# q norm and layer norm: two channel tiles added before the ones-matmuls, and a short last key tile in the first query half

## The chip, the cores and the metric

The kernel runs on one core of a Trainium2 chip, in one launch. Its time is that of the device, in microseconds (us), the median of several runs. A core has five engines with queues of their own: PE (TensorE, matmuls), DVE (VectorE), ACT (ScalarE), POOL (GpSimd) and SP (SyncE, which here only issues DMAs). PE reads SBUF and writes PSUM; it runs a matmul as a weight load (the stationary operand, "PEld" in the profile) and a pass of the moving operand.

## The reference

One layer of a hybrid decoder: 16 meta tokens are put ahead of 1024 tokens of width 1024, one input projection feeds four token mixers, their outputs are gated and merged, and an output projection is added to the residual. Float32 throughout. What the change touches are three pieces of it:

```python
# multi-head latent attention: norm of the low-rank query (256 channels), causal softmax
q = (rms_norm(c_q, q_norm_g) @ w_uq).reshape(b_, l_, MLA_HEADS, QK_NOPE + QK_ROPE)
...
s = jnp.where(k_pos[None, :] <= q_pos[:, None], s, -jnp.inf)
p = jax.nn.softmax(s, axis=-1)

# Conformer convolution module (256 channels)
z = causal_dwconv(z, w_dw) + b_dw
z = layer_norm(z, ln_g, ln_b)
```

`rms_norm` divides by the root of the mean of squares over the channels; `layer_norm` first takes the mean over the channels off.

## The kernel before

Most matrices lie with channels on the 128 partitions and tokens along the free dimension, so 256 channels are two tiles, and the 1024 tokens are worked in two halves of 512 (`c` = 0, 1). A float32 product is made of three matmuls of high and low parts (`split` makes these: ACT copies the high part, POOL or DVE subtracts it).

**Stage one** is the input projection, in units of seven block products each (tiles `ps_pa` to `ps_pd`; operands `A`, `S` from the weights, `B`, `T` from the input). `prep` turns the next weights into such operands (tiles `raw`, `ss`, `S`, `A` on DVE, ACT and POOL). Between the products, `pump` lets four "lanes" of smaller tasks take steps: the convolutions, the query and key/value tasks (`task_q`, `task_kv`), the short convolution, layer norm and pooling (`task_short`, `task_norm`, `task_pool`), and the output weights (`task_w`). `task_norm(1)` is the last task of its lane. Its last stores (`store_bo`, tile `cgt`, with `bohi`) are the last DMAs that SP issues for the stage.

**Column sums.** Sums over channels run across partitions, so PE makes them with a vector of ones. `rs_row` (line 849) takes a list `sqs` of tiles of squares, makes for each 128 tokens a matmul with the squares as the stationary operand and the ones as the moving one (one column), with all tiles of the list accumulated in one PSUM group; DVE scales, POOL takes the power -1/2 (tile `rs`), and PE transposes the result back into a row over all partitions. `task_q` (tile `sqq`, each half once) and `task_norm` (tile `lsq`, each half once) call it with two tiles, `task_kv` with one. `task_norm` also needs the sum of the values themselves: the convolution's output is loaded into two tiles `lacc`, and two matmuls of 512 columns, with ones as weights, put the sum on all partitions (`pa`). DVE takes the mean off `lacc`, ACT squares the result into `lsq`. Its tiles come from a ring of four (`t2`).

**Stage two** is attention, head by head and half by half, with the output products of the other three mixers as filling work (tiles `whl`, `bo`, `th`, `ps_y`). `maxima` makes a bound for each query's scores. `attend` (line 1330) goes over tiles of 128 keys, `nj` = 5 in the first half and 9 in the second: three score matmuls with the keys as weights (`ps_s`), the causal mask on DVE, exp on ACT (`p`), a split (`pt`), three value matmuls (`ps_o`). Keys count the 16 meta tokens, so the last tile of either half meets only the last 16 queries of the half. **Stage three** is the product of attention's output and the output projection.

**Order.** Every operation is recorded first, with a cost from a small model; `Plan.flush` then simulates the engines and writes out an order for each, once for each stage. An operation is taken when its inputs are planned to be ready and its buffers free, in the order of recording, where some (`plan.ahead`) are lifted. Loads and stores are given planned landing times, with some microseconds more inside `plan.slow`. The hardware keeps that order on each engine and waits where the plan was too early. The cost of a matmul in the model goes by its free size and not by the number of keys. All operations are issued in `issue`, so the profile shows line 330 for them; its groups are told apart by tile names.

Of the kernel before, what the change touches and what calls it, by code (L numbers as in the profile page):

```python
# [30 lines left out]
P = 128  # L31
D = 1024
NT = 1024
NM = 16
# [30 lines left out]
def f(ap):  # L65
    return ap.bitcast(F32)
# [369 lines left out]
def trunk_kernel(ctx, tc, a):  # L436
    nc = tc.nc
    plan = Plan(nc)
    PE, ACT, DVE, POOL, SP = (plan.engine(e) for e in ("PE", "ACT", "DVE", "POOL", "SP"))
# [7 lines left out]
    def ld(out, in_):  # L447
        SP.dma_start(f(out) if out.dtype == F32R else out, f(in_) if in_.dtype == F32R else in_)

    def copy(out, in_, scale=1.0):  # L450
        ACT.activation(out, in_, AF.Copy, scale=scale)
# [4 lines left out]
    def add(eng, out, x, y):  # L456
        eng.tensor_tensor(out, x, y, op=ALU.add)

    def mul(eng, out, x, y):
        eng.tensor_tensor(out, x, y, op=ALU.mult)  # L460

    def split(hi, lo, src, eng=None):
        copy(hi, src)
        sub(eng or POOL, lo, src, f(hi))
# [5 lines left out]
    ones = const.tile([P, 1], F32, name="ones")  # L470
# [44 lines left out]
    def bank(tag="x"):  # L515

        return psum.tile([P, 512], F32, tag=tag, bufs=2 if tag == "x" else 1, name=f"ps_{tag}")
# [10 lines left out]
    def t2(shape, dt=F32, name="t2"):  # L528
        return tp.tile(shape, dt, tag="t2", bufs=4, name=name)
# [4 lines left out]
    def col(shape, name):  # L534
        return tp.tile(shape, F32, tag=name, bufs=2 if name == "rs" else 1, name=name)
# [313 lines left out]
    def rs_row(sqs, of, scale=None, tag="x"):  # L849

        n = sqs[0].shape[1]
        p = min(n, P)
        pc = bank(tag)[:p, :n // p]
        for j in range(n // p):
            for i, sq in enumerate(sqs):
                PE.matmul(pc[:, j:j + 1].in_order(), sq[:, p * j:p * (j + 1)], ones, start=(i == 0),
                          stop=(i == len(sqs) - 1), skip_group_check=True)  # L860
        yield
        rs = col([P, 4], "rs")[:p, :n // p]
        DVE.tensor_scalar(rs, pc, 1.0 / of, EPS, op0=ALU.mult, op1=ALU.add)
        POOL.tensor_tensor(rs, rs, mhalf[:p, :n // p], op=ALU.pow)
        if scale:
            DVE.tensor_scalar(rs, rs, scale, None, op0=ALU.mult)
        yield
        out = bank(tag)[:, :n]
        for j in range(n // p):
            PE.transpose(out[:, p * j:p * (j + 1)], rs[:, j:j + 1].to_broadcast([p, P]), ident[:p, :p])  # L870
        yield
        return out
# [28 lines left out]
    def store_bo(i, c, src):  # L901

        s_ = slice(512 * c, 512 * (c + 1))
        hi, lo = t2([P, 512], F32R, name="bohi"), src.bitcast(F32R)
        split(hi, lo, src)
        ld(bo_dram[i][:, 0, s_], hi)
        ld(bo_dram[i][:, 1, s_], lo)

    def task_norm(c):

        s_ = slice(512 * c, 512 * (c + 1))
        acc = [t2([P, 512], name="lacc") for m in range(2)]
        for m in range(2):
            ld(acc[m], acc_dram[m][:, s_])
        pa = bank("y")
        for m in range(2):
            PE.matmul(pa, ones.to_broadcast([P, P]), acc[m], start=(m == 0), stop=(m == 1))
        yield
        sq = [t2([P, 512], name="lsq") for m in range(2)]
        for m in range(2):  # L920
            DVE.scalar_tensor_tensor(acc[m], pa, -1.0 / 256.0, acc[m], op0=ALU.mult, op1=ALU.add)
            ACT.activation(sq[m], acc[m], AF.Square)
        yield
        rs = yield from rs_row(sq, 256, tag="y")
        for m in range(2):
            g, b, hb = (t_[:, r + m:r + m + 1] for t_, r in ((par, R_LG), (par, R_LB), (par, R_HLB)))
            DVE.scalar_tensor_tensor(acc[m], acc[m], g, rs, op0=ALU.mult, op1=ALU.mult)
            th, cg = t2([P, 512], name="lth"), t2([P, 512], name="cgt")
            ACT.activation(th, acc[m], AF.Tanh, scale=0.5, bias=hb)
            ld(cg, z_dram[f"cg{m}"][:, s_])  # L930
            DVE.tensor_scalar(acc[m], acc[m], b, 0.5, op0=ALU.add, op1=ALU.mult)
            DVE.scalar_tensor_tensor(acc[m], th, 1.0, acc[m], op0=ALU.add, op1=ALU.mult)
            yield
            mul(POOL, cg, acc[m], cg)
            store_bo(2 + m, c, cg)
            yield
# [72 lines left out]
    def task_q(c):  # L1009
# [4 lines left out]
        for m in range(2):  # L1014
            ld(cq[:, m], z_dram[f"cq{m}"][:, s_])
            ACT.activation(sq[:, m], cq[:, m], AF.Square)
        yield
        rs = yield from rs_row([sq[:, 0], sq[:, 1]], 256, QK ** -0.5)
        ch = []
        for m in range(2):  # L1020
# [63 lines left out]
    def task_kv():  # L1084
# [20 lines left out]
        for n0, n in CH_KV:  # L1105
            rs = yield from rs_row([sq[:, n0:n0 + n]], P)
            DVE.scalar_tensor_tensor(ckv[:, n0:n0 + n], ckv[:, n0:n0 + n], par[:, R_KVG:R_KVG + 1], rs,
                                     op0=ALU.mult, op1=ALU.mult)
# [60 lines left out]
    def lane(*tasks):  # L1169

        for needs, task, *args in tasks:
# [3 lines left out]
            while True:  # L1175
# [10 lines left out]
             ): 0.8,  # L1186
        lane(*[((f"b{m}", f"c{m}", f"x{m}", f"sg{m}"), task_short, m, c) for m, c in halves]
             + [(("conv00", "conv10", "cg0", "cg1"), task_norm, 0)]
             + [((f"pv{m}", f"pg{m}"), task_pool, m, c) for m, c in halves]
             + [(("conv01", "conv11"), task_norm, 1)]): 1.1,  # L1190
        lane(*[((), task_w, n, i, c) for n in w_dram for i in range(len(w_dram[n][0])) for c in range(KD)]): 0.5,
    }
# [137 lines left out]
    def attend(h, c):  # L1330

        q_, k_, v_ = qt[h, c], kt[h % 2], vt[h % 2]
        po = bank("o")
        nj = 4 * c + 5
        for j in range(nj):
            lo_ = max(512 * c, P * j - NM)
            n = 512 * (c + 1) - lo_
            kn = P if j < 8 else NM
            ks = slice(P * j, P * j + kn)
            qs = slice(512 - n, 512)  # L1340
            s = bank("s")[:kn, :n]
            PE.matmul(s, k_[:NA, 0, ks], q_[:NA, 0, qs], start=True, stop=False)
            PE.matmul(s, k_[:QK, 0, ks], q_[:QK, 1, qs], start=False, stop=False)
            PE.matmul(s, k_[:QK, 1, ks], q_[:QK, 0, qs], start=False, stop=True)
            d0 = P * j - NM
            dl, dh = max(d0, 512 * c, 0), min(d0 + P, 512 * (c + 1))
            if dh > dl:
                sd = s[:, dl - lo_:dh - lo_]
                add(DVE, sd, sd, maskT[:kn, dl - d0:dh - d0])
            p32 = at.tile([P, 512], F32, tag="p32", bufs=3, name="p32")[:kn, :n]  # L1350
            pt_ = at.tile([P, 2, 512], F32R, tag="pt", bufs=4, name="pt")[:kn, :, :n]
            ACT.activation(p32, s, AF.Exp)
            split(pt_[:, 0], pt_[:, 1], p32)
            o = po[:, lo_ - 512 * c:]
            PE.matmul(o, v_[:kn, j, :P], pt_[:, 0], start=(j == 0), stop=False, skip_group_check=True)
            PE.matmul(o, v_[:kn, j, :P], pt_[:, 1], start=False, stop=False, skip_group_check=True)
            PE.matmul(o[:64], v_[:kn, j, P:], pt_[:, 0], start=False, stop=(j == nj - 1), skip_group_check=True)
            yield
        if c == 0:
            ol[h] = at.tile([P, 2, 512], F32, tag="ol", bufs=2, name="ol")  # L1360
        copy(ol[h][:, c], po)
# [111 lines left out]
    for i, (h, c) in enumerate(seq):  # L1473
        with plan.behind():
            if i + 2 < len(seq):
                load_q(*seq[i + 2])
            if c == 0 and h + 1 < H:
                load_kv(h + 1)
            if c == 0 and h % 2:
                smg[h] = at.tile([P, NT], F32, tag="smg", name="smg")  # L1480
                ld(smg[h], z_dram[f"mg{h // 2}"])
        for _ in attend(h, c):
            units += 1
            lead_to(-1, min(5 + units * 10 / 14, 5 * (i + 3)))
            refill()
        lead_to(i + 1)

        with plan.ahead(300 if h == H - 1 else 0):
            if h == H - 1:
                head_out(h, c, sums_pe(h, c))  # L1490
            elif c:
                for k, rb in enumerate(sums(h)):
                    head_out(h, k, rb)
# [233 lines left out]
```

## Time and profile before

| | |
|---|---|
| runs, us | 1011.25, 1011.64, 1013.38 (median 1011.64) |
| profiled execution: first to last instruction (span), us | 1010.7 |
| mean granted clock of TensorE | 0.993 |
| DMA over the span | 203.13 MB, 201 GB/s |

The time that the profiled execution takes besides its span isn't in the profile; the median of the runs is 0.9 us above the span. Times in the profile are microseconds from the first instruction, those of one instruction nanoseconds. A group has the form "out<-in", with shapes (partitions x elements; for PE contraction rows*weight columns first), a count, busy time and mean, and idle time ahead of it with what ended it. "PE busy" counts a pass from its start to its modelled end, so passes overlap, and the distance between starts says more about their cost. Stage one ends near 660 us, attention lies from there to 876 us, stage three after that.

### The profile page before, as it was taken

The numbers are of one execution on the slowest core, as the hardware profiler recorded it, in microseconds if no ns is written. First come the engines' busy times: TensorE is split into PE (matmuls) and PEld (weight loads), VectorE is DVE, ScalarE is ACT, GpSimd is POOL, SyncE is SP. The second block draws the span as 40 slices with busy tenths as digits, with TensorE's granted clock in tenths as the row PEclk, the third lists the DMA queues.
The fourth block names the chain that finished last, engine by engine and source line by source line (L and its number), as shares of the span: only waits on it lengthen the run. The fifth ranks groups of instructions, "written<-read, shape, count | busy, mean of one in ns | idle before, by whom it ended". The sixth has DMA issues, their size and how long they took to land.

```text
span 1010.7 us, 15256 instructions
## 1 busy us (share of the span) xinstructions
PE 988.6 (98%) x5129; PEld 831.5 (82%) x5129; DVE 683.4 (68%) x1106; ACT 444.6 (44%) x895; POOL 680.8 (67%) x634
## 2 busy tenths in 40 slices
PE   9999999999999999999999999999999999999996
PEld 9999898889888877878778778867888788788885
DVE  6846794897789679645435444265777777898547
ACT  7633233443434455435444434225565656224632
POOL 6768766577575696777668645334569796647946
PEclk9999999999999999999999999998999999999998
DMA  7269656568676866955654643795857672673634
GB/s 247 75 211 308 231 162 194 185 206 287 204 263 214 293 185 206 299 181 159 205 178 158 190 143 115 229 348 174 242 158 245 185 230 75 247 251 99 192 98 166
DMA packets 126302, 203.13 MB, mean 201 GB/s; under 512 B 19650, under 2 KB 79161, under 8 KB 124880
## 3 DMA queue, kind: packets, MB, share of 16 engines
q1 hardware_dynamic: 121600, 185.38, 58.0%
q10 hardware_dynamic: 4336, 15.73, 4.2%
q8 instruction: 40, 0.66, 0.3%
q0 software_dynamic: 288, 1.05, 0.3%
q14 instruction: 38, 0.31, 0.1%
HBM read 128.40 MB, written 73.72 MB: 200 GB/s over the span
## 4 chain that ended last, share of the span: by engine, by line
PE 83%; DMA 5%; POOL 4%; DVE 4%; issue 3%; ACT 0%; SPq 0%; DVEq 0%; POOLq 0%; ACTq 0%
PE ps_pb L330 15%; PE ps_pa L330 14%; PE ps_pc L330 13%; PE ps_o L330 10%; PE ps_u L330 7%; PE ps_s L330 7%; PE ps_pd L330 6%; PE ps_y L330 6%; PE ps_x L330 4%; PE ps_w L330 1%; DMA vt<-v 1%; DMA th<-th 1%; POOL S L330 1%; DMA kt<-kr 1%; DVE op L330 1%
## 5 line engine op out<-in xcount | busy, mean ns | idle before, releaser
L330 PE MATMUL ps_pb<-T,S 128*128 128x512 f32 (+2 forms) x792 | 174.2, 363 | 0.1
L330 PE MATMUL ps_pa<-B,A 128*128 128x512 f32 (+2 forms) x792 | 172.0, 361 | 0.0
L330 POOL TENSOR_TENSOR S<-ss,S 128x512 fp32r<-128x512 f32 x84 | 114.2, 1370 | 73.4 <-ACT S L330 72.4
L330 PEld LDWEIGHTS ps_pa<-B,A 128*128 128x128 f32 x792 | 134.7, 188 | 23.9
L330 PEld LDWEIGHTS ps_pb<-T,S 128*128 128x128 f32 x792 | 133.7, 188 | 24.8 <-issue 1.7
L330 POOL TENSOR_TENSOR A<-raw,A 128x512 fp32r<-128x512 f32 x84 | 115.0, 1378 | 42.7 <-ACT A L330 42.5
L330 POOL TENSOR_TENSOR pt<-p,pt 128x512 fp32r<-128x512 f32 (+4 forms) x112 | 102.6, 942 | 48.7 <-PE ps_s L330 28.6
L330 DVE SCALAR_TENSOR_TENSOR ps_w<-conv,par,ps_w 128x512 f32<-128x512 f32 x116 | 87.3, 752 | 2.6
L330 PE MATMUL ps_pc<-T,S 128*128 128x512 f32 (+2 forms) x396 | 87.8, 363 | 0.5 <-DVE z L330 0.5
L330 PE MATMUL ps_pd<-T,A 128*128 128x512 f32 (+2 forms) x396 | 86.0, 362 | 0.0
L330 PE MATMUL ps_pc<-B,S 128*128 128x512 f32 (+2 forms) x396 | 85.8, 362 | 0.0
L330 PE MATMUL ps_y<-bo,whl 128*128 128x512 f32 x288 | 83.1, 407 | 0.6 <-DVE m L330 0.4
L330 ACT ACTIVATE p<-ps_s 128x512 f32<-128x512 f32 (+4 forms) x112 | 49.7, 444 | 73.8 <-PE ps_s L330 29.0
L330 ACT ACTIVATE S<-ss 128x512 fp32r<-128x512 f32 x84 | 51.0, 628 | 69.7 <-DVE ss L330 39.9
L330 PEld LDWEIGHTS ps_pc<-B,S 128*128 128x128 f32 x396 | 67.3, 188 | 12.3 <-issue 0.5
L330 PEld LDWEIGHTS ps_pd<-T,A 128*128 128x128 f32 x396 | 67.2, 188 | 11.9
L330 PEld LDWEIGHTS ps_pc<-T,S 128*128 128x128 f32 x396 | 66.7, 188 | 12.4 <-DVE z L330 0.7
L330 PE MATMUL ps_o<-pt,vt 128*128 128x512 f32 (+4 forms) x336 | 73.8, 335 | 1.8 <-ACT ol L330 1.6
L330 PE MATMUL ps_s<-qt,kt 100*128 100x512 f32 (+4 forms) x336 | 68.5, 330 | 0.7 <-DVE qt L330 0.7
L330 ACT ACTIVATE A<-raw 128x512 fp32r<-128x512 f32 x84 | 52.3, 625 | 35.6 <-PE ps_pd L330 19.3
L330 PEld LDWEIGHTS ps_o<-pt,vt 128*128 128x128 f32 x336 | 52.7, 175 | 15.1 <-ACT ol L330 3.2
L330 PEld LDWEIGHTS ps_s<-qt,kt 100*128 100x128 f32 x336 | 56.1, 183 | 10.7 <-issue 0.9
(341 smaller groups left out, 1895.1 us busy)
## 6 DMA issues: line engine op xcount, KB each, us to landing
raw<-in_w_in_dram SPq DMA_DIRECT2D x56, 512.0 KB
th<-th SPq DMA_DIRECT2D x32, 512.0 KB
th<-z ACTq DMA_DIRECT2D x30, 512.0 KB
v<-vhl SPq DMA_DIRECT2D x16, 384.0 KB
qt<-q SPq DMA_DIRECT2D x16, 384.0 KB
bo<-bo SPq DMA_DIRECT2D x6, 1024.0 KB
vt<-v SPq DMA_DIRECT2D x8, 768.0 KB
kt<-k SPq DMA_DIRECT2D x8, 520.0 KB
```

Of the source, the lines that this page charges most:

```text
L330: getattr(self.handle[o["eng"]], o["op"])(*map(real, o["args"]), **{k: real(v) for k, v in o["kw"].items()})
```

## The change

Three edits. `rs_row` adds the second tile of squares to the first on POOL where there are two, and makes its one-column matmuls on the sum alone; `task_norm` adds the two tiles of values on POOL into a tile that it later uses for the first squares, and makes one channel-sum matmul; and `attend` takes 16 keys in the last tile of either half, where it took 16 in that of the second half only.

```diff
@@ rs_row
         p = min(n, P)
+        if len(sqs) > 1:
+            add(POOL, sqs[0], sqs[0], sqs[1])
+        sq = sqs[0]
         pc = bank(tag)[:p, :n // p]
         for j in range(n // p):
-            for i, sq in enumerate(sqs):
-                PE.matmul(pc[:, j:j + 1].in_order(), sq[:, p * j:p * (j + 1)], ones, start=(i == 0),
-                          stop=(i == len(sqs) - 1), skip_group_check=True)
+            PE.matmul(pc[:, j:j + 1].in_order(), sq[:, p * j:p * (j + 1)], ones, start=True, stop=True,
+                      skip_group_check=True)
@@ task_norm
+        sq = [t2([P, 512], name="lsq")]
+        add(POOL, sq[0], acc[0], acc[1])
         pa = bank("y")
-        for m in range(2):
-            PE.matmul(pa, ones.to_broadcast([P, P]), acc[m], start=(m == 0), stop=(m == 1))
-        yield
-        sq = [t2([P, 512], name="lsq") for m in range(2)]
+        PE.matmul(pa, ones.to_broadcast([P, P]), sq[0], start=True, stop=True)
+        yield
+        sq.append(t2([P, 512], name="lsq"))
@@ attend
-            kn = P if j < 8 else NM
+            kn = P if j < nj - 1 else NM
```

## The prediction

> **What bounds the kernel now.** I read the page first: busy times, slices, chain.
>
> ```profile
> span 1010.7 us, 15256 instructions
> PE 988.6 (98%) x5129; PEld 831.5 (82%) x5129; DVE 683.4 (68%) x1106; ACT 444.6 (44%) x895; POOL 680.8 (67%) x634
> PE 83%; DMA 5%; POOL 4%; DVE 4%; issue 3%; ACT 0%; SPq 0%; DVEq 0%; POOLq 0%; ACTq 0%
> ```
>
> TensorE (PE) is busy for 988.6 of 1010.7 us and carries 83% of the chain that ended last. Whole-span shares can hide stages, so the next view is the busy time by stretch, cut at the places that the change touches.
>
> ```profile
> 355.00:375.00 20.00, 19.99 (x94) 15.57 (x93) 13.71 (x21) 10.76 (x21) 18.16 (x15) 1.00 0.60 196
> 375.00:400.00 25.00, 23.76 (x113) 19.35 (x112) 24.33 (x34) 12.41 (x24) 18.53 (x19) 1.00 0.64 183
> 465.00:485.00 20.00, 20.00 (x96) 16.25 (x95) 10.50 (x14) 9.71 (x18) 14.09 (x16) 1.00 0.51 162
> 585.00:620.00 35.00, 35.00 (x159) 28.11 (x158) 18.02 (x25) 15.59 (x26) 19.69 (x15) 1.00 0.31 101
> 680.00:690.00 10.00, 6.33 (x26) 5.45 (x27) 4.00 (x12) 1.63 (x6) 2.25 (x5) 0.66 0.64 165
> 700.00:800.00 100.00, 98.58 (x546) 83.42 (x544) 75.34 (x188) 59.34 (x135) 73.42 (x87) 1.00 0.75 224
> ```
>
> After the stretch and its length stand PE, weight loads, DVE, ACT and POOL, then the granted clock. The change sits in 355-400 (q norm and layer norm of the first half), 465-485 (q norm, second half), 585-620 (layer norm, second half) and, with its key tile, in attention from 676 on. PE is full in all of them. So PE time that goes should come off the end, unless something else becomes late. The candidates are POOL in 355-375 (18.16 of 20), DVE in 375-400 (24.33 of 25), and the change of stages near 680, the one row above in which PE stood (6.33 of 10) and the clock fell (0.66).
>
> **The change part by part.** *Column sums.* Each `rs_row` over two tiles issues 8 one-column matmuls; the trace has each as two passes, so 16. In order of time for the second layer norm (start, us, tile, count):
>
> ```profile
> 594.60 0.28 PE L330 MATMUL ps_y<-ones,lsq 128*128 128x1 f32 x2
> 594.74 0.71 PE L330 MATMUL ps_pd<-T,A 128*128 128x512 f32 x2
> 595.29 1.62 PE L330 MATMUL ps_y<-ones,lsq 128*128 128x1 f32 x14
> 596.77 0.48 PE L330 MATMUL ps_pd<-T,A 128*128 128x512 f32 x1
> 597.08 2.03 PE L330 MATMUL ps_pc<-B,S 128*128 128x512 f32 x8
> 598.95 0.60 PE L330 MATMUL ps_y<-ident,rs 128*128 128x128 f32 x4
> ...
> 636.61 2.79 PE ps_pc L330 x12
> ```
>
> The last row, of the chain, gives the normal pass: 2.79/12 = 0.232 us. From 594.60 to 598.95 are 4.35 us with 11 of those (2.55), which leaves 1.80 for 16 one-column passes: 0.112 each. Eight fewer in each of four calls: 32 x 0.112 = **3.6 us** off PE.
>
> *Sum over channels in the layer norm.* Two full-width fp32 matmuls, four passes, become one:
>
> ```profile
> 588.16 1.02 PE L330 MATMUL ps_y<-lacc,ones 128*128 128x512 f32 x2
> 588.62 1.26 PE L330 MATMUL ps_pb<-T,S 128*128 128x512 f32 x3
> 589.72 2.50 PE L330 MATMUL ps_pa<-B,A 128*128 128x512 f32 x10
> ```
>
> From 588.16 to 589.72 are 1.56 us with three normal passes (0.70): 0.43 for each sum pass. Two fewer in two calls: 4 x 0.43 = **1.7 us**.
>
> *Key tile.* For the first query half, j = 4 is the last tile. Its 128 keys held 16 that a query may see; now it has those 16. The second half's j = 8 already has this form, so one trace shows both, here by the weight loads:
>
> ```profile
> 678.61 0.51 PEld L330 LDWEIGHTS ps_s<-qt,kt 100*128 100x128 f32 x3
> 679.05 0.19 PEld L330 LDWEIGHTS ps_s<-kt,qt 96*128 96x128 f32 x1
> ...
> 697.45 0.36 PEld L330 LDWEIGHTS ps_s<-qt,kt 100*16 100x16 f32 x3
> 697.74 0.19 PEld L330 LDWEIGHTS ps_y<-bo,whl 128*128 128x128 f32 x1
> ...
> L330 PEld LDWEIGHTS ps_o<-pt,vt 16*128 16x128 f32 x16 | 2.5, 182 | 1.0 <-issue 0.2
> L330 POOL TENSOR_TENSOR pt<-p,pt 16x16 fp32r<-16x16 f32 x8 | 2.2, 269 | 0.1
> L330 POOL TENSOR_TENSOR pt<-p,pt 128x16 fp32r<-128x16 f32 x8 | 1.7, 218 | 0.0
> ```
>
> The three score loads take 0.44 us until the next one with 128 keys and 0.29 with 16: 0.15 a head, 8 heads, **1.2 us**. The value matmuls gain nothing: their weights stay 128 wide (182 ns at 16 keys). POOL's split is no shorter either (269 against 218 ns), and ACT and DVE work on the same 16 columns, so I take zero there; PE covers it, and uncovered it would be 8 x 0.05 us. The Trainium skill, "TensorE: Matmul & The Clock Gate", section LDWEIGHTS, has a load cost its columns over 1.2 a ns, whatever the contraction length; worked out, an estimate, that is 0.093 us less a load, 2.2 us over 24. The trace agrees on the value loads and shows about half on the score loads; by the page the sum would be 1.0 us lower.
>
> *What is added.* Six POOL additions of 128x512 (one in each `rs_row`, one ahead of each channel sum). Nearest rows, forms that POOL runs now on two fp32 tiles:
>
> ```profile
> L330 POOL TENSOR_TENSOR cgt<-lacc,cgt 128x512 f32<-128x512 f32 x4 | 5.7, 1415 | 0.0
> L330 POOL TENSOR_TENSOR m<-m,t 128x512 f32<-128x512 f32 x4 | 6.9, 1730 | 0.6 <-DVE t L330 0.6
> ```
>
> About 1.4 us each, 8 us on an engine with 330 us free: nothing by itself. Queued behind them on POOL are the `S`, `A` and `whl` splits of coming weights and the `rs` power. But each adds a place where PE's fixed order can wait for POOL, and behind a waiting column sum stand all products of the unit. How often such a place waits now:
>
> ```profile
> PE ps_x L330 <- POOL rs L330: 1.5, 2, 0.8
> PE ps_x L330 <- POOL cqn L330: 0.8, 1, 0.8
> PE ps_y L330 <- POOL rs L330: 0.5, 1, 0.5
> ```
>
> There are 7 powers and 4 `cqn` splits that PE needs, and they cost it 2.8 us: 0.25 each. Six more: **1.5 us**; bounds are none and six of the longest, 4.8. The written order comes from the planner, which moves the sums later by the addition's cost, so I stay at the mean.
>
> *What is moved.* The layer norm's later steps go back by two additions and forward by the PE time saved there; with them its last two stores, on SP's queue, ahead of all loads of the next stage:
>
> ```profile
> 639.22 0.32 SPq L330 DMA_DIRECT2D bo<-bohi  x1
> ...
> 640.97 0.42 SPq L330 DMA_DIRECT2D qt<-q  x1
> ...
> 655.91 2.95 PE L330 MATMUL ps_pc<-B,S 128*128 128x512 f32 x12
> ...
> SPq L330 <- ACT bohi L330: 18.4, 1, 18.4
> SPq L330 <- PE ps_pc L330: 1.2, 1, 1.2
> PE ps_s L330 <- DMA kt<-kr: 3.7, 1, 3.7
> ```
>
> SP stood 18.4 us for that store's value, then issued attention's loads. PE begins the last group of products of the stage at 655.91. If the loads start at the same moment while PE is done 3.8 us earlier (3.6 + 1.7 - 1.5), PE waits for them. Bounds: nothing lost (the loads move along: from the first `bo` on some wait for tiles that PE's last products free, 1.2 us for `ps_pc` in the rows) and all 3.8. By these gates the larger part moves along; I take **0.6**.
>
> Sum: -3.6 - 1.7 - 1.2 + 1.5 + 0.6 = -4.4 us. The profiled span of 1010.7 becomes 1006.3; the median of the runs, 1011.64, lies 0.9 above the span for what surrounds it, so the forecast is **1007.2**. A measurement of this kernel tells about 0.2%, 2 us, from no change: 1009.6 to 1013.7 is "same".
>
> **The rivals.** *1. The change of stages swallows it.* For: the SP rows above, and a DMA share of 0.97 where the loads start, which leaves them no room to catch up:
>
> ```profile
> 640.00:650.00 10.00, 10.00 (x45) 8.12 (x44) 0.81 (x2) 1.39 (x3) 1.82 (x2) 1.00 0.97 265
> ```
>
> Against: PE's own releases gate some of the loads. All 3.8 us lost leaves the key tile, -1.2; two additions minus the PE time saved put the layer norm's end about 0.9 later: 1010.4 to 1011.3, say 1011.
>
> *2. The same stall turns slow (slower).* If PE stands there for longer than the 3.7 us after which the clock row shows 0.66, another 10 us go at that clock: 10 x 0.34 = 3.4 us on top of rival 1: **1014.4**. It decides from a second stall of that length; the 0.8 us of the waits listed above left 375-400 at 1.00.
>
> *3. POOL and DVE crowd in 355-400.* Three of the six additions fall there. An addition in step between two DVE operands can stretch DVE:
>
> ```profile
> L330 DVE SCALAR_TENSOR_TENSOR lacc<-lth,lacc x4: 693/1670/1780, 391.5 to 618.6; 128x512 f32<-128x512 f32 x4
> PE ps_pc L330 <- DVE z L330: 0.5, 1, 0.5
> ```
>
> The same operation takes 693 to 1780 ns, 1.09 more at the worst; three times that, all on PE, is +3.3: 1010.5. Against: PE waited for DVE's `z` once, for 0.5 us. The Trainium skill, "SBUF — State Buffer", section Who interferes with whom, speaks against the change here: of a DVE operation with two SBUF inputs and a GpSimd operation, the second to start is blocked for all of the first. The row's 693 and 1780 agree with it.
>
> *4. The stall at 680 goes.* The changed times may order `kt`'s load earlier. It costs 3.7 us, and of the 3.4 lost to the clock 3.7 x 0.5 = 1.8 lie in the wait itself, so 1.6 more: 5.3 less than forecast, 1001.9.
>
> **How the numbers follow.** Forecast 0.54 (from 1005.1, with no new wait and nothing lost, to 1009.6, with 3.9 us of waits for POOL); rival 1 0.18; rival 2 0.13; rival 3 0.07; rival 4 0.08. Faster: 0.54 + 0.08 = 0.62; same: 0.18 + 0.07 = 0.25; slower: 0.13. The range reaches up over rivals 1 and 3 to just short of rival 2 and down to 1003.5, halfway from the forecast's lower end to rival 4: 1003.5 to 1013.5 leaves out rivals 2 and 4 at most.
>
> **What would show it.** Right: 32 `sqq`/`lsq` passes instead of 64, 4 `lacc` passes instead of 8, score loads of 16 columns 48 instead of 24, PE busy lower by some 6 us, six POOL additions near 1.4 us, PE's waits for them together under 2 us, and SP's first `qt` load some 4 us earlier than 640.97. Wrong: that load at 641 or later with PE idle between 655 and 685 grown by 4 us (rival 1), a second stretch of clock 0.66 (rival 2), PE waits for DVE `u` or `z` in 355-400 (rival 3).

## The result, and the profile after

| | before | after |
|---|---|---|
| runs taken together, us | median 1011.44 (1011.11 to 1013.38, 4 runs) | median 1006.22 (1005.0 to 1008.12, 4 runs) |
| span of the profiled execution, us | 1010.7 | 1005.5 |
| stage one, to the first matmul of `maxima`, us | 658.7 | 652.0 |
| attention, from there to the first `ps_u`, us | 219.3 | 221.0 |
| stage three, from there to the end, us | 132.7 | 132.5 |

The ratio of the runs is 0.9942 (95% interval 0.9928 to 0.9956), so the changed kernel is faster by 0.6%. The prediction was 1007.2 us.

The cuts of the table are these rows of PE's timeline (start, us, then the group). Before:

```profile
658.70 0.70 PE L330 MATMUL ps_s<-kt,qt 96*128 96x144 f32 x4
...
877.96 1.41 PE L330 MATMUL ps_u<-boM,whl 128*128 128x512 f32 x5
```

After:

```profile
652.04 0.70 PE L330 MATMUL ps_s<-kt,qt 96*128 96x144 f32 x4
...
873.00 6.29 PE L330 MATMUL ps_u<-boM,whl 128*128 128x512 f32 x26
```

Stage one gained 6.7 us, and attention, where the key tile lies, gave back 1.7. The page of after, first lines and chain:

```profile
span 1005.5 us, 15187 instructions
PE 985.0 (98%) x5093; PEld 828.5 (82%) x5093; DVE 679.9 (68%) x1106; ACT 445.8 (44%) x895; POOL 689.3 (69%) x640
PE 90%; DVE 4%; issue 2%; POOL 2%; DMA 1%; ACT 0%; SPq 0%; DVEq 0%; POOLq 0%; ACTq 0%
```

PE has 36 passes fewer, POOL six instructions and 8.5 us more, and PE's share of the chain rose from 83% to 90%. Busy time by stretch (PE, weight loads, DVE, ACT, POOL, then clock, DMA share, GB/s):

```profile
355.00:400.00 45.00, 45.00 (x207) 36.50 (x206) 38.42 (x55) 23.28 (x45) 41.93 (x35) 1.00 0.61 182
465.00:485.00 20.00, 20.00 (x86) 15.91 (x85) 8.44 (x12) 8.69 (x16) 16.15 (x17) 1.00 0.69 210
670.00:680.00 10.00, 6.42 (x28) 4.93 (x28) 5.50 (x17) 3.61 (x10) 3.71 (x6) 0.81 0.92 224
680.00:690.00 10.00, 10.00 (x36) 8.07 (x35) 4.52 (x11) 5.28 (x10) 3.44 (x3) 0.68 0.18 54
```

In 355-400 POOL is now busy for 41.93 of 45 us, and PE is full there, where before it stood for 1.24 us (23.76 of 25 in 375-400). The weak place is the old one: two rows with a clock under 1, where before had one (0.66). They lose 10 x 0.19 + 10 x 0.32 = 5.1 us against 3.4.

The groups of after that the change touches (count | busy us, mean ns | idle before):

```profile
L330 PE MATMUL ps_x<-ones,sqq 128*128 128x1 f32 x16 | 1.9, 239 | 0.0
L330 PE MATMUL ps_y<-ones,lsq 128*128 128x1 f32 x16 | 1.9, 240 | 0.0
L330 PE MATMUL ps_y<-lsq,ones 128*128 128x512 f32 x4 | 2.0, 591 | 0.0
L330 POOL TENSOR_TENSOR lsq<-lsq 128x512 f32<-128x512 f32 x2 | 2.6, 1304 | 1.8 <-ACT lsq L330 1.8
L330 POOL TENSOR_TENSOR lsq<-lacc 128x512 f32<-128x512 f32 x2 | 2.6, 1292 | 0.0
L330 POOL TENSOR_TENSOR sqq<-sqq 128x512 f32<-128x512 f32 x2 | 2.6, 1291 | 0.0
```

32 one-column passes instead of 64, four channel-sum passes instead of eight, and six additions of 1.29 to 1.30 us. The mean of 239 ns is a modelled end, longer than what a pass costs; the starts give that, here for the second q norm:

```profile
494.50 0.94 PE L330 MATMUL ps_x<-ones,sqq 128*128 128x1 f32 x8
495.31 2.33 PE L330 MATMUL ps_pa<-B,A 128*128 128x512 f32 x9
497.47 0.86 PE L330 MATMUL ps_pd<-T,A 128*128 128x512 f32 x3
```

From 494.50 to 497.47 are 2.97 us; nine products at 0.232 take 2.09, which leaves 0.88 for 8 passes: 0.11 each, as forecast.

And the waits. In 160-655 us, before had PE waiting for POOL's `cqn` (0.8 us, at 380) and `rs` (0.5, at 383), and 0.2 for DVE's `vhl`. After has two of 0.2 us there, neither for an added tile; the third row is the one stall left in attention:

```profile
PE ps_x L330 <- POOL whl L330: 0.2, 1, 0.2
PE ps_x L330 <- DVE vhl L330: 0.2, 1, 0.2
...
PE ps_s L330 <- DMA kt<-kr: 3.3, 1, 3.3
```

None of the six additions made PE wait, and two old waits went.

### The profile page after: what moved, and what is told of

The parts are those of the page before. It is cut to its first block, busy times and chain, and to the rows that moved or that the text cites. A ratio compares the mean times of both kernels' runs of the same rounds, so it can differ in the third digit from the quotient of the medians.

```text
span 1005.5 us, 15187 instructions
## 1 busy us (share of the span) xinstructions
PE 985.0 (98%) x5093; PEld 828.5 (82%) x5093; DVE 679.9 (68%) x1106; ACT 445.8 (44%) x895; POOL 689.3 (69%) x640
## 4 chain that ended last, share of the span: by engine, by line
PE 90%; DVE 4%; issue 2%; POOL 2%; DMA 1%; ACT 0%; SPq 0%; DVEq 0%; POOLq 0%; ACTq 0%
PE ps_pb L330 16%; PE ps_pa L330 15%; PE ps_pc L330 15%; PE ps_o L330 10%; PE ps_pd L330 7%; PE ps_u L330 7%; PE ps_s L330 7%; PE ps_y L330 7%; PE ps_x L330 4%; PE ps_w L330 1%; DVE op L330 1%; DMA kt<-kr 1%; DVE ps_w L330 1%; DVE a L330 1%; POOL S L330 0%
## 5 line engine op out<-in xcount | busy, mean ns | idle before, releaser
L330 PEld LDWEIGHTS ps_o<-pt,vt 128*128 128x128 f32 (+1 forms) x336 | 53.2, 174 | 16.1 <-ACT ol L330 3.3
L330 PEld LDWEIGHTS ps_s<-qt,kt 100*128 100x128 f32 (+1 forms) x336 | 55.2, 179 | 11.5 <-issue 0.9
```

The source lines that it names most:

```text
L330: getattr(self.handle[o["eng"]], o["op"])(*map(real, o["args"]), **{k: real(v) for k, v in o["kw"].items()})
```

## The experiments

The first theory was that the passes taken off PE are the gain, that the additions are hidden, and that attention gave back time after the stall for `kt`. The rivals were that the additions cost something, that the key tile is what attention lost by, and that the stall is not involved. Every ratio is against the kernel before on the same chip in the same batch (medians of 1012.25, 1012.21 and 1012.59 us).

| run | what it is | median, us (range, runs) | ratio to before |
|---|---|---|---|
| e1_colsum | `rs_row` edit alone | 1006.74 (1006.05 to 1007.01, 5) | 0.9944 (0.9931 to 0.9957) |
| e2_chansum | `task_norm` edit alone | 1008.88 (1007.94 to 1012.1, 12) | 0.9976 (0.9964 to 0.9988) |
| e3_key | key tile alone | 1014.16 (1010.68 to 1016.98, 12) | 1.0013 (0.9998 to 1.0028) |
| e4_adds_full_passes | after, each sum made twice | 1014.68 (1010.55 to 1016.89, 12) | 1.0018 (1.0004 to 1.0031) |
| e5_no_adds | after without the additions | 1005.39 (1004.33 to 1008.4, 6) | 0.9924 (0.9904 to 0.9944) |
| after_again | after, beside e5 and e11 | 1006.16 (1005.55 to 1008.14, 6) | 0.9931 (0.9912 to 0.9949) |
| e9_sums_only | after without the key tile | 1004.61 (1003.08 to 1008.0, 6) | 0.9923 (0.9906 to 0.9941) |
| e6_after_kt1_early | after, `kt` of the second head loaded earlier | 1003.1 (1001.26 to 1006.01, 6) | 0.9912 (0.9892 to 0.9933) |
| e6_again | the same, beside e11 | 1003.0 (1000.99 to 1003.95, 6) | 0.9897 (0.9876 to 0.9918) |
| e11_sums_kt1_early | e6 without the key tile | 1003.79 (1003.46 to 1004.44, 6) | 0.9906 (0.9889 to 0.9924) |
| e7_before_kt1_early | before, `kt` loaded earlier | 1022.27 (1020.45 to 1023.93, 5) | 1.0093 (1.0075 to 1.0111) |
| e10_key_kt1_early | e7 with the key tile | 1022.26 (1020.28 to 1022.75, 5) | 1.0089 (1.0072 to 1.0106) |

### The three edits one by one

e1 has the column sums alone:

```diff
+        if len(sqs) > 1:
+            add(POOL, sqs[0], sqs[0], sqs[1])
+        sq = sqs[0]
...
-            for i, sq in enumerate(sqs):
-                PE.matmul(pc[:, j:j + 1].in_order(), sq[:, p * j:p * (j + 1)], ones, start=(i == 0),
-                          stop=(i == len(sqs) - 1), skip_group_check=True)
+            PE.matmul(pc[:, j:j + 1].in_order(), sq[:, p * j:p * (j + 1)], ones, start=True, stop=True,
+                      skip_group_check=True)
```

> Column sums alone: rs_row adds the two tiles of squares on POOL and makes half the one-column matmuls; the channel sum and the key tile are as before. By passes (PE time that goes comes off the end): 32 passes of 0.112 us, -3.6 us against before, between -2.5 and -5.5 with the waits for POOL. By order (the gain is the planner's new order, whose waits of 1.2 us on PE in 375-400 went and whose layer norm came earlier): anything from -1 to -6, and not in the proportion of the passes.

e2 has the channel sum alone:

```diff
+        sq = [t2([P, 512], name="lsq")]
+        add(POOL, sq[0], acc[0], acc[1])
         pa = bank("y")
-        for m in range(2):
-            PE.matmul(pa, ones.to_broadcast([P, P]), acc[m], start=(m == 0), stop=(m == 1))
+        PE.matmul(pa, ones.to_broadcast([P, P]), sq[0], start=True, stop=True)
```

> Channel sum alone: task_norm adds the two value tiles on POOL and makes one sum matmul. By passes: 4 passes of 0.43 us, -1.7 us against before, between -0.5 and -3. By order: as much as the column sums alone give, or nothing.

e3 has the key tile alone:

```diff
-            kn = P if j < 8 else NM
+            kn = P if j < nj - 1 else NM
```

> Key tile alone: the last key tile of the first half has 16 keys. The planner's model has the same cost for it, so the order is that of before. By passes: 24 weight loads that each take 0.05 us less, -1.2 us, up to -2.2. By order: nothing, within 0.5 us of before.

The column sums alone give nearly all of the change's gain: 0.56% of 1012 is 5.7 us, for passes worth 3.6. Its profile says where the rest is: stage one is 3.95 us shorter (`maxima` begins at 654.75, before at 658.70), and attention is 2.4 shorter (216.8 against 219.3), because the stall for `kt` described below is 2.1 us long instead of 3.7 and the half clock behind it 3.4 instead of 6.8. The channel sum alone gives 2.4 us (1.7 of passes), though its profile shows no gain at all in stage one (`maxima` begins at 658.87): the two waits below are 1.9 us where before had 1.3, and a wait for DVE's `z` at 139 us, ahead of the edit, is 1.3 us longer than in before. Its runs lie near 1011.9 us (4, the profiled one among them, at a mean clock of 0.993) and near 1008.6 (8, at 0.995 to 0.996), so part of the 2.4 may be the clock's. PE's waits of e2 in 160-655:

```profile
PE ps_y L330 <- POOL rs L330: 1.0, 1, 1.0
PE ps_x L330 <- DVE rs L330: 0.9, 1, 0.9
```

So what an addition costs in waits is not a sum of fixed prices: each edit makes the planner write another order, and that order has 1.9 us of such waits with two additions and none with six. The key tile alone is not faster: its ratio reaches from 0.9998 to 1.0028, where the prediction had it 1.2 us faster (0.9988).

### Are the additions hidden, and are the passes the gain?

e4 keeps everything of the change and gives PE its passes back:

```diff
-            PE.matmul(pc[:, j:j + 1].in_order(), sq[:, p * j:p * (j + 1)], ones, start=True, stop=True,
-                      skip_group_check=True)
+            for i in range(len(sqs)):
+                PE.matmul(pc[:, j:j + 1].in_order(), sq[:, p * j:p * (j + 1)], ones, start=True, stop=True,
+                          skip_group_check=True)
...
-        PE.matmul(pa, ones.to_broadcast([P, P]), sq[0], start=True, stop=True)
+        for i in range(2):
+            PE.matmul(pa, ones.to_broadcast([P, P]), sq[0], start=True, stop=True)
```

> All three edits, with the six additions, but each column-sum and channel-sum matmul on the added tile is made twice (the second overwrites the first with the same), so that PE has as many passes in stage one as before. By passes: only the key tile is left, -1.2 us, and whatever the additions cost, up to +1.5: -2 to +1 against before. By order: most of the gain stays, -3 to -5.

e5 leaves the additions out, so that half of the squares and of the values is missing from the sums:

```diff
-        if len(sqs) > 1:
-            add(POOL, sqs[0], sqs[0], sqs[1])
         sq = sqs[0]
...
-        add(POOL, sq[0], acc[0], acc[1])
         pa = bank("y")
-        PE.matmul(pa, ones.to_broadcast([P, P]), sq[0], start=True, stop=True)
+        PE.matmul(pa, ones.to_broadcast([P, P]), acc[0], start=True, stop=True)
```

> The changed kernel without the six additions: the column sums and the channel sum are made of the first tile alone, so half of the squares and values are left out of them. If the additions are hidden (theory, and the forecast's lower end): within 1.5 us of the changed kernel. If they cost PE what the forecast took for them: 1.5 us faster; if they cost the whole of POOL's 8 us: up to 8 us faster.

With the passes back, the gain is gone (1.0018). Without the additions, the kernel runs 0.8 us faster than after on the same chip, with intervals that overlap widely and would allow some 3 us. The profiles say more: counted from one group of products ahead of the first addition (the `ps_pa` group that begins at 351.46 us in before), stage one of e5 is 0.3 us shorter than that of after and after_again. Of the 7.8 us of six additions, that is what reaches its end. e4 has waits of its own in 160-655, in the same two places as e2: 1.3 us for POOL's `rs` and 0.9 for DVE's. It adds 5.3 us of passes and these 2.2 us to after, 7.5 together; its stage one ends 7.6 us later than that of after (659.60 against 652.04), and the medians, on two chips, lie 8.5 apart.

Passes and waits make up stage one in all of them. Counted from the same `ps_pa` group, it is 6.9 us shorter than before in after, 4.2 shorter in e1, 0.8 shorter in e2 and 1.0 longer in e4. The passes taken off and PE's waits in 160-655 (1.5 us before; 0.4, 0.8, 2.1 and 2.4) make 6.4, 4.3 and 1.1 shorter and 0.9 longer.

### The stall, and the clock behind it

The longest wait of PE in attention is for the keys of the second head (`kt`). What it costs beyond itself is seen in the same passes, in the same order, of both kernels. Each fence has the first pass after the wait (with the wait in brackets), a later group, and the end of the sequence. Before:

```profile
684.59 0.78 PE L330 MATMUL ps_s<-kt,qt 96*128 96x144 f32 x2 [3.67 <-DMA kt<-kr]
690.26 2.74 PE L330 MATMUL ps_s<-qt,kt 100*128 100x512 f32 x11
692.83 0.40 PE L330 MATMUL ps_o<-pt,vt 128*128 128x512 f32 x1
```

After:

```profile
676.95 0.78 PE L330 MATMUL ps_s<-kt,qt 96*128 96x144 f32 x2 [3.30 <-DMA kt<-kr]
683.59 4.03 PE L330 MATMUL ps_s<-qt,kt 100*128 100x512 f32 x11
687.45 0.40 PE L330 MATMUL ps_o<-pt,vt 128*128 128x512 f32 x1
```

8.24 us became 10.50: the group of eleven score passes took 2.57 us from start to start before and 3.86 after, because the clock came back later. These windows are cut where the half clock begins and ends (columns as above), first before, then after:

```profile
682.58:689.40 6.82, 4.82 (x19) 4.49 (x20) 1.38 (x4) 0.60 (x1) 0.00 (x0) 0.50 0.57 171
676.22:686.46 10.24, 9.52 (x30) 8.10 (x31) 5.06 (x13) 1.84 (x4) 0.00 (x0) 0.50 0.33 94
```

The half clock lasted 3.4 us longer, and 0.7 us of it instead of 2.0 lay in the wait, so PE worked through 9.52 us of it instead of 4.82. Half of the difference is the 2.3 us, which is more than attention gave back. The wait itself didn't grow. SP's `kt` loads for the second head, which the prediction feared for, moved along with PE (the first began at 672.95 before), though the first `qt` load went 26 us ahead, from 640.97. In the timeline of SP's queue after:

```profile
614.85 0.42 SPq L330 DMA_DIRECT2D qt<-q  x1
665.63 0.48 SPq L330 DMA_DIRECT2D kt<-k  x1
```

Those 26 us are room that after doesn't use. e6 uses it, by issuing the second head's loads right behind the first's; e7 does the same in before:

```diff
     load_kv(0)
     load_q(*seq[1])
+    load_kv(1)
...
-            if c == 0 and h + 1 < H:
+            if c == 0 and 0 < h < H - 1:
```

> The changed kernel with the second head's keys and values loaded right behind the first head's, ahead of the fills' loads. If the key tile's gain is lost to the clock after PE's wait for kt (theory): that wait of 3.3 us and the half-clock stretch near 680 both go, 3.3 + 9.5 x 0.5 = 8 us at most, less what the later fill loads cost: -4 to -8 against the changed kernel, about 1000, and runs closer together. If the wait only moves to another load (rival): within 2 us of the changed kernel, 1004 to 1008.

> The kernel before with the same early load. There SP's loads begin at 641 and not at 615, with the DMA engines full from then on: 1.3 MB more ahead of the fills' loads is some 3 us at 400 GB/s. Theory: the wait of 3.7 us and its half clock go (-5), the fills' loads come later (+1 to +3): -2 to -4 against before. Rival (the early load only trades one wait for another): -1 to +3.

In e6 the stall and the low clock near 680 are both gone, and it is the fastest kernel here: 1003.0 against 1006.16 us of after on the same chip. In the profiles of these two, attention is 4.4 us shorter (215.5 against 219.9), but stage three 1.3 longer (134.1 against 132.8), because a half clock of 3.4 us now lies at 867, behind waits of 1.6 and 1.0 us at the end of attention. The first of them and the stretch, from e6_again:

```profile
865.17 0.43 PE L330 MATMUL ps_y<-ident,ol 64*128 64x64 f32 x4 [1.56 <-DVE th L330]
...
865.00:870.00 5.00, 3.85 (x15) 3.07 (x16) 3.44 (x6) 0.08 (x1) 2.16 (x2) 0.67 0.45 174
```

In before the same edit costs 9 to 10 us, since there SP begins these loads at 641 and they push others back: its first load of a fill's weights (`whl`) goes from 643.78 to 657.39. The longest of PE's waits in e7:

```profile
PE ps_y L330 <- DMA whl<-w_out_pool: 9.9, 1, 9.9
```

And the stretch of e7 in which it lies (columns as above):

```profile
660.00:670.00 10.00, 0.14 (x1) 0.00 (x0) 0.89 (x4) 0.45 (x1) 4.61 (x11) 0.62 0.99 389
```

PE did 0.14 us of work in 10, with the DMA share at 0.99. So rivals 1 and 2 of the prediction describe something that this kernel does do, under another edit.

### The key tile by itself

If the stall hides what the key tile is worth, it should show without the stall, or with the other edits in place. e9 is after without the key tile (`kn = P if j < 8 else NM` again); e10 puts the key tile on e7; e11 is e6 without it.

> The changed kernel without the key tile edit, everything in the same order. Theory (the key tile lengthens the half-clock stretch by one 3.4 us window): at or below the changed kernel, 1004 to 1006.5, with a mean clock of 0.994 or more. Rival (the key tile saves its 1.2 us as predicted, and the longer stretch was chance): 1.2 us above the changed kernel.

> The kernel before with the early load and the key tile edit, to be set beside the one with the early load alone. Theory: with no wait there is no half clock to lengthen, and the key tile gives its 24 shorter weight loads, -1 to -2 us. Rival (the key tile itself is slower, in PE or in the work behind it): 0 to +2 us.

> The early load and the two sums without the key tile edit, beside the same kernel with it (next run): PE doesn't wait for kt there, so the clock after that wait can't hide the key tile. If the key tile saves its 24 x 0.05 us: 1 to 2 us slower than with it. If it saves nothing (the score loads lie behind other work of the tile): equal within 0.7 us.

> The changed kernel with the early load, again, on the chip of the other three: 1001 to 1006, 3 us below the changed kernel.

> The changed kernel again, for the comparison on one chip: 1005 to 1008, ratio to before 0.993 to 0.996.

The medians point both ways: with the key tile the kernel is slower than e9 (by 1.5 us in the medians, which come from two chips, and by 0.8 in the ratios), and 0.8 us faster than e11 (intervals overlap in both pairs); e10 equals e7, and their stalls of 9 to 10 us drown the question. The trace settles the direct part. e11 and e6_again run nearly the same order, and this stretch has the last score tile (`100x16`) and the last value tile of one head's first half. The timeline of PE in e11, with 128 keys in both:

```profile
758.87 0.44 PE L330 MATMUL ps_y<-bo,whl 128*128 128x512 f32 x1
759.15 0.40 PE L330 MATMUL ps_s<-qt,kt 100*128 100x16 f32 x3
759.40 0.48 PE L330 MATMUL ps_y<-bo,whl 128*128 128x512 f32 x1
...
763.88 0.52 PE L330 MATMUL ps_o<-pt,vt 128*128 128x144 f32 x5
764.25 0.71 PE L330 MATMUL ps_y<-bo,whl 128*128 128x512 f32 x2
```

And in e6_again, with 16 in both (the row `16*128` comes from a narrower window: it is the last three passes of the row above it; so are the rows `128x16` and `16*128` in the fence of before further down):

```profile
758.79 0.44 PE L330 MATMUL ps_y<-bo,whl 128*128 128x512 f32 x1
759.07 0.23 PE L330 MATMUL ps_s<-qt,kt 100*16 100x16 f32 x3
759.15 0.48 PE L330 MATMUL ps_y<-bo,whl 128*128 128x512 f32 x1
...
763.62 0.67 PE L330 MATMUL ps_o<-pt,vt 128*128 128x144 f32 x5
763.85 0.44 PE L330 MATMUL ps_o<-pt,vt 16*128 16x16 f32 x3
764.22 0.72 PE L330 MATMUL ps_y<-bo,whl 128*128 128x512 f32 x2
```

The score tile went from 0.25 to 0.08 us, start to start: 0.17 less. The value tiles, two passes of 144 queries and three of 16 in both kernels, went from 0.37 to 0.60: 0.23 more. The trace of before has both forms too, first half (128 keys) and second half (16 keys) of a head, and shows where it lies:

```profile
728.77 0.52 PE L330 MATMUL ps_o<-pt,vt 128*128 128x144 f32 x5
728.91 0.39 PE L330 MATMUL ps_o<-pt,vt 128*128 128x16 f32 x3
729.15 0.56 PE L330 MATMUL ps_s<-kt,qt 96*128 96x400 f32 x2
...
771.69 0.61 PE L330 MATMUL ps_o<-pt,vt 128*128 128x144 f32 x4
771.92 0.44 PE L330 MATMUL ps_o<-pt,vt 16*128 16x16 f32 x3
772.29 0.47 PE L330 MATMUL ps_s<-kt,qt 96*128 96x456 f32 x1
```

0.38 against 0.60 us. The three passes of 16 queries take 0.37 instead of 0.24 (771.92 to 772.29, 728.91 to 729.15), and the two passes of 144 queries ahead of them, with 128 rows in both, 0.23 instead of 0.14: the second is slower where weights of 16 rows follow. (The first of the three passes of 144 queries lies further ahead, between other products.) It doesn't look like a wait for data, whose length would vary: in all five heads of before in which three 16-key passes stand together, they take 0.37. Over the eight heads, from before to after, the score tiles save 0.13 to 0.21 us each, 1.5 together, and the value tiles lose 0.22 each (0.28 in the first, at half clock), 1.8 together: the key tile costs PE about 0.3 us by itself. e3 and e9 go the same way. In the profiles, attention of e6_again is 0.7 us shorter than that of e11 (215.5 and 216.2), which is less than one wait of PE for DVE's `mx` that e11 has and neither profile of the e6 kernel. PE's waits in e11:

```profile
PE ps_s L330 <- DVE mx L330: 0.9, 1, 0.9
```

## Why the prediction came out right

The time is within 1 us of the forecast, and the main terms, the passes taken off PE, are confirmed. That it is so close is luck in part: the waits for POOL and the change of stages came out 3.6 us better than forecast, and the key tile and the clock behind the stall 3.8 us worse.

- **Column sums, −3.6, and channel sum, −1.7.** Confirmed: 0.11 us a pass, half the passes, and no gain without them (e4). Together with the next term they make nearly all of stage one's 6.7 us: 5.3 of passes, and 1.1 of waits that went (1.5 us in 160-655 before, 0.4 after).
- **New waits for POOL, +1.5.** The wrong size: none of the six places waited, and the waits for `cqn` and `rs` that before had are gone. The step was to take the mean of the old waits for each new one; the waits depend on the order that the planner writes, and e2 and e4 had 1.9 and 2.2 us of them. The bounds that the prediction gave (none, and 4.8) left out a gain, though its own rows had one to give: it called PE full in all stretches of the change, but in 375-400 PE worked 23.76 of 25 us, and the 1.24 are the waits for `cqn` and `rs` that went. The two longer waits for `rs` (at 148 and 152 us) and the one for `z` (at 139), which it also used, lie outside these stretches.
- **Additions, nothing by themselves.** Confirmed: 1.3 us each, hidden behind PE's products but for 0.3 us of the 7.8 (e5).
- **Key tile, −1.2.** Wrong, and the step that failed is "the value matmuls gain nothing: their weights stay 128 wide". It took the loads' durations (182 ns with 16 keys, 0.19 us with 128) for the passes' cost, and not the starts, by which the value passes cost 0.22 us more a head with 16 keys. The score part was right in kind (0.13 to 0.21 a head, forecast 0.15). The Trainium skill, "TensorE: Matmul & The Clock Gate", section LDWEIGHTS, has a load cost the same whatever the contraction length. The durations of the loads agree; the time of the passes, which that rule doesn't price, is what grew.
- **Change of stages, +0.6.** It cost nothing: `kt`'s loads came 7.3 us earlier (665.63 against 672.95), PE came to them 7.3 us earlier (it began to wait at 673.65, before at 680.92), and the wait is 3.3 instead of 3.7. The first `qt` load moved by 26 us where about 4 were forecast; PE waits for the first head's loads in neither kernel, so this gave after nothing, but it is what e6 lives on.
- **Not in the sum:** PE worked longer at the low clock behind the stall, +2.3 us. Of these, 0.28 are the value passes, which take 1.00 instead of 0.72 us at that clock. With them, PE's busy time fell by 3.6 us, and not by some 6 as forecast.

So attention's +1.7 is made of +2.3 behind the stall, some 0.2 for the key tile in the other heads, −0.4 of the stall itself, and −0.4 for a wait (`ps_y` for DVE's `m`) that after doesn't have. Against the forecast, stage one is 2.9 us better than −3.8, attention 2.3 worse than −1.2 + 0.6, and the two nearly cancel.

Rival 1 (the change of stages swallows the gain) and rival 2 (a second stall) did not happen, nor did rival 3: POOL at 93% in 355-400 made PE wait for nothing. Rival 4 did not happen by itself; e6 made it happen by hand, and was worth 3.2 us of the 5.3 forecast for it, with 1.3 lost again at the end of attention.

**What stays open.** Why the low clock lasted longer. In the profiles with the key tile and the stall, the sequence above took 10.50, 9.13, 10.27, 10.02 and 9.76 us (after, after_again, e5, e3, e4); without the key tile 8.24, 7.59, 8.46 and 7.56 (before, e1, e2, e9). The two sets don't overlap. The half clock itself lasts 10.2 us in after, e5, e3 and e4 and 6.8 in after_again; without the key tile it lasts 6.8 in before and e2 and 3.4 in e1 and e9. The mean clocks of all runs go the same way: against before in the same batch, they are up to 0.0009 lower with key tile and stall (after_again, e5, e4, e3) and 0.0006 to 0.0019 higher without the key tile (e9, e1, e2), where 0.001 is about 1 us. So the key tile seems to cost time through the clock as well; but the wait ahead differs in each profile (2.1 to 3.7 us), the half clock begins earlier or later in it, and whether the slower passes hold the clock down was not tried. Nor is it shown why a pass with 16 rows of weights takes longer than one with 128.

## What to carry to other kernels

Where PE bounds a stage, adding tiles on an engine with room and summing once is worth the passes that it takes off PE, priced from start to start, and whatever the new order does to PE's waits (here from 1.1 us less to 0.9 more). Price a smaller tile in the same way, in both products that use it: a shape that shortens one load can lengthen the other's passes, and often the trace of before already has both shapes. After a gain, look again at the stall that is left: an earlier load order that cost 9 to 10 us in the kernel before was worth 3 us in the kernel after, because the change had freed the queue ahead of it.

## What the runs showed of the hardware that was not expected

- Three value passes of 16 queries take 0.37 us with weights of 16 rows and 0.24 with weights of 128 rows, and the two passes with 128 rows just ahead of them 0.23 instead of 0.14 us (before, 771.69 and 728.77). At the low clock it is the same way round (the groups of five: 1.00 against 0.72 us).
- A wait of PE of 2.1 to 3.7 us is followed by half clock for a time that differs from profile to profile, even of one kernel (10.2 and 6.8 us in two profiles of after; the same passes took 10.50 and 9.13). Two shorter waits 0.4 us apart, of 1.6 and 1.0 us, were followed by it too (e6_again). The windows of after in steps of 5 us (PE busy, clock, DMA share, GB/s) show the clock at 0.50 while PE is full:

```profile
675.00:680.00 5.00, 3.06 (x11) 0.62 0.82 246
680.00:685.00 5.00, 5.00 (x17) 0.50 0.01 2
685.00:690.00 5.00, 5.00 (x21) 0.85 0.36 105
```

The Trainium skill, "TensorE: Matmul & The Clock Gate", section What's actually happening, has the clock either full or half, and a warm-up of about 3.4 us. The 0.50 agrees. The length agrees in e1 and e9 alone (3.4 us): the clock lost in these three rows is (0.38 + 0.50 + 0.15) x 5 = 5.15 us, which at half clock is 10.3 us, three times as long, with PE at work for 9.5 of it.
